# Batch norm on one core: a second DMA ring for the stores, parameters fetched as rows, and a last tile in two halves

## The chip, the cores and the metric

The kernel runs on one core of one Trainium2 chip. The metric is the device time of one execution in microseconds (us). The figure for the kernel before is the median of ten executions. The profile and the trace come from one of them, which has a time of its own.

## What is computed

The reference is batch normalisation with stored statistics over an input of 32 x 256 x 128 x 128 in float32:

```python
mean = running_mean.reshape(1, -1, 1, 1)
var = running_var.reshape(1, -1, 1, 1)
return gamma * (x - mean) / np.sqrt(var + eps) + beta
```

Each of 256 channels has one scale, gamma / sqrt(var + eps), and one shift, beta - mean * scale. The output is x * scale + shift, element by element. `x` is 537 MB and the output is as large, so 1074 MB pass through the core.

## The kernel before

The 256 channels are cut into two blocks of 128, one channel to a partition. With 32 images this makes 64 tiles of 128 x 16384 float32, 8.39 MB each, 64 KB in a partition. `xr[i]` and `outr[i]` are tile i in the input and in the output; tile i uses column i % 2 of the scales and shifts.

Three buffers of that size (`NBUF`, a pool of the tile framework, tag `t`) hold tiles. A tile is loaded into one, `compute` rewrites it in place on VectorE with one `tensor_scalar` (times scale, plus shift), and `store` writes it out from there. The framework places the semaphores: a load into a used buffer waits for the store that empties it, a `compute` for its load, a store for its `compute`.

Loads (line 48) and stores (line 97) are all issued by SyncE (SP), so they share one queue of the DMA hardware, in the order in which the program issues them. First come loads 0, 1 and 2. Then a loop goes over pairs of tiles (K = NBUF - 1 = 2):

```python
for i in idxs:
    compute(i)
for i in idxs:
    store(i)
for i in idxs:
    issue_load(i + NBUF)
```

SP's order is therefore L0 L1 L2, S0 S1, L3 L4, S2 S3, L5 L6 and so on (L a load, S a store), ending with L63, S62, S63.

The four parameter vectors of 256 values are fetched by four DMAs issued by GpSimd (POOL, line 56), each rearranged so that a partition gets its two channels' values: elements of 4 bytes. ScalarE takes the square root (line 71, with a table load ahead of it), VectorE the reciprocal, two products and a difference (lines 78 to 81). These give `scale_t` and `shift_t`, which tile 0 waits for.

Of the kernel before, what the change touches and what calls it, by code (L numbers as in the profile page):

```python
# [1 line left out]

# [4 lines left out]


SINGLE_QUEUE = True  # L10
NBUF = 3


@with_exitstack
def kernel(
    ctx: ExitStack,
    tc: tile.TileContext,
    x: bass.AP,
    gamma: bass.AP,
    beta: bass.AP,  # L20
    running_mean: bass.AP,
    running_var: bass.AP,
    out: bass.AP,
):
    nc = tc.nc
    eps = 1e-5

    N, C, H, W = x.shape
    P = nc.NUM_PARTITIONS
    assert C % P == 0  # L30
    NCB = C // P
    HW = H * W
    NT = N * NCB

    params = ctx.enter_context(tc.tile_pool(name="params", bufs=1))
    data = ctx.enter_context(tc.tile_pool(name="data", bufs=NBUF))

    xr = x.rearrange("n (cb p) h w -> (n cb) p (h w)", p=P)
    outr = out.rearrange("n (cb p) h w -> (n cb) p (h w)", p=P)

    tiles = {}
    loads = {}

    def issue_load(i):
        if i >= NT:
            return
        t = data.tile([P, HW], mybir.dt.float32, tag="t")
        loads[i] = nc.sync.dma_start(out=t[:], in_=xr[i])  # L48
        tiles[i] = t

    for i in range(NBUF):
        issue_load(i)

    def load_param(ap_1d):
        t = params.tile([P, NCB], mybir.dt.float32, tag=ap_1d.tensor.name)
        nc.gpsimd.dma_start(out=t, in_=ap_1d.rearrange("(j p) -> p j", p=P))  # L56
        return t

    var_t = load_param(running_var)
    gamma_t = load_param(gamma)  # L60
    beta_t = load_param(beta)
    mean_t = load_param(running_mean)

    eps_t = params.tile([P, 1], mybir.dt.float32, tag="eps")
    nc.vector.memset(eps_t, eps)  # L65

    scale_t = params.tile([P, NCB], mybir.dt.float32, tag="scale")
    shift_t = params.tile([P, NCB], mybir.dt.float32, tag="shift")
    tmp_t = params.tile([P, NCB], mybir.dt.float32, tag="tmp")

    nc.scalar.activation(  # L71
        out=tmp_t[:],
        in_=var_t[:],
        func=mybir.ActivationFunctionType.Sqrt,
        bias=eps_t[:],
        scale=1.0,
    )
    nc.vector.reciprocal(out=tmp_t[:], in_=tmp_t[:])  # L78
    nc.vector.tensor_mul(out=scale_t[:], in0=gamma_t[:], in1=tmp_t[:])  # L79
    nc.vector.tensor_mul(out=tmp_t[:], in0=mean_t[:], in1=scale_t[:])  # L80
    nc.vector.tensor_sub(out=shift_t[:], in0=beta_t[:], in1=tmp_t[:])  # L81

    def compute(i):
        t = tiles[i]
        cb = i % NCB
        nc.vector.tensor_scalar(  # L86
            out=t[:],
            in0=t[:],
            scalar1=scale_t[:, cb : cb + 1],
            scalar2=shift_t[:, cb : cb + 1],  # L90
            op0=mybir.AluOpType.mult,
            op1=mybir.AluOpType.add,
        )

    def store(i):
        t = tiles.pop(i)
        (nc.sync if SINGLE_QUEUE else nc.scalar).dma_start(out=outr[i], in_=t[:])  # L97

    K = NBUF - 1
    for b in range((NT + K - 1) // K):  # L100
        idxs = [i for i in range(K * b, K * b + K) if i < NT]
        for i in idxs:
            compute(i)
        for i in idxs:
            store(i)
        for i in idxs:
            issue_load(i + NBUF)


# [1 line left out]
_INS = ['x', 'gamma', 'beta', 'running_mean', 'running_var']  # L111
_OUTS = [((32, 256, 128, 128), 'float32')]


# [23 lines left out]
```

## Time and profile before

| | |
|---|---|
| median of ten executions | 2487.51 us (2486.53 to 2491.59) |
| the profiled execution's own time | 2486.91 us |
| its span in the profile | 2484.9 us |
| moved by DMA in the span | 1073.77 MB, 432 GB/s on average |
| `tensor_scalar` on VectorE, 128 x 16384 | 64 times, 8812 ns each |
| a load, from issue to landing (median) | 38.6 us |
| a store, from issue to landing (median) | 49.8 us |
| the four parameter fetches, from issue to landing | 10.9, 15.4, 19.7 and 21.7 us |

The span runs from the first to the last instruction that the profile counts; the execution's own time is 2.0 us longer, and the median of the ten is 0.6 us above that execution. The time from issue to landing contains the time in which a transfer stands in the queue behind others, so it is longer than the transfer itself. The page's row "GB/s" has one number for each fortieth of the span (62.1 us). In the chain of waits, a piece is named for the work whose end released the next step.

### The profile page before, as it was taken

Reading aid. Unit: us, or ns where it says so; the run is one execution under the profiler, and the core shown is the slowest. Engines: PE = TensorE matmul, PEld = TensorE weight load, DVE = VectorE, ACT = ScalarE, POOL = GpSimd, SP = SyncE. Lnnn points to the kernel's source line nnn. Section 1 sums busy time; section 2 is a strip of 40 time slices with the busy share of each in tenths; the row PEclk is TensorE's granted clock in tenths of the full one; section 3 lists DMA queues with packets and bytes.
Section 4 is the critical chain, followed back from the end, with each engine's and each line's share of the span. In section 5 each row is a group of like instructions: output and inputs, shape, how many; then the busy total and the mean of one; then the engine's idle time right before and its main releaser. Section 6 shows DMA issues by size and latency. Waiting matters only on the chain.

```text
span 2484.9 us, 378 instructions
## 1 busy us (share of the span) xinstructions
DVE 564.7 (23%) x69; ACT 1.6 (0%) x2; POOL 3.2 (0%) x8
## 2 busy tenths in 40 slices
DVE  2122211222112221122212222121221212222121
ACT  0000000000000000000000000000000000000000
POOL 0000000000000000000000000000000000000000
DMA  9999999999999999999999999999999999999999
GB/s 410 434 436 430 431 433 435 433 434 428 435 436 437 427 438 436 428 434 437 435 429 436 435 431 436 436 435 428 437 435 430 435 436 431 436 436 436 430 434 400
DMA packets 18562, 1073.77 MB, mean 432 GB/s; under 512 B 2176, under 2 KB 2176, under 8 KB 2176
## 3 DMA queue, kind: packets, MB, share of 16 engines
q1 hardware_dynamic: 18432, 1073.75, 99.9%
q0 software_dynamic: 128, 0.00, 0.0%
q14 instruction: 2, 0.02, 0.0%
HBM read 536.88 MB, written 536.87 MB: 432 GB/s over the span
## 4 chain that ended last, share of the span: by engine, by line
DMA 51%; another core or an unknown queue 36%; DVE 11%; SPq 0%; issue 0%; POOL 0%; DVEq 0%; POOLq 0%; PEldq 0%
DMA t<-in_x_dram 48%; DVE t L86 11%; DMA out_dram<-t 2%; DMA t<-in_running_mean_dram 1%; SPq L97 0%; POOL t L56 0%; DVEq L86 0%; POOLq L133 0%; SPq L48 0%; DVE shift_t L81 0%; DVE tmp_t L80 0%; DVEq L80 0%; PEldq L133 0%
## 5 line engine op out<-in xcount | busy, mean ns | idle before, releaser
L86 DVE TENSOR_SCALAR t<-t,scale_t,shift_t 128x16384 f32<-128x16384 f32 x64 | 564.0, 8812 | 1864.7 <-DMA t<-in_x_dram 1864.6
L78 DVE RECIPROCAL tmp_t<-tmp_t 128x2 f32<-128x2 f32 x1 | 0.2, 167 | 12.9 <-ACT tmp_t L71 12.9
L80 DVE TENSOR_TENSOR tmp_t<-t,scale_t 128x2 f32<-128x2 f32 x1 | 0.2, 161 | 7.5 <-DMA t<-in_running_mean_dram 7.5
L71 ACT ACT_TABLE_LOAD x1 | 1.3, 1283 | 12.2 <-DMA t<-in_running_var_dram 12.2
L79 DVE TENSOR_TENSOR scale_t<-t,tmp_t 128x2 f32<-128x2 f32 x1 | 0.2, 161 | 3.6 <-DMA t<-in_gamma_dram 3.6
L56 POOL DMA_DIRECT2D t<-in_running_var_dram x1 | 0.8, 837 | 0.8 <-PEq L133 0.8
L56 POOL DMA_DIRECT2D t<-in_gamma_dram x1 | 0.7, 722 | 0.0
L56 POOL DMA_DIRECT2D t<-in_beta_dram x1 | 0.7, 722 | 0.0
L56 POOL DMA_DIRECT2D t<-in_running_mean_dram x1 | 0.7, 722 | 0.0
L71 ACT ACTIVATE tmp_t<-t,eps_t 128x2 f32<-128x2 f32 x1 | 0.3, 297 | 0.0
L65 DVE MEMSET eps_t<- 128x1 f32 x1 | 0.1, 59 | 0.8 <-PEq L122 0.8
L81 DVE TENSOR_TENSOR shift_t<-t,tmp_t 128x2 f32<-128x2 f32 x1 | 0.2, 162 | 0.0
L122 POOL MEMSET const-bfloat16-1.0<- 128x1 bf16 x1 | 0.1, 96 | 0.0
L122 POOL MEMSET const-float32-0.0<- 128x1 f32 x1 | 0.1, 93 | 0.2 <-issue 0.2
L122 POOL MEMSET const-float32-1.0<- 128x1 f32 x1 | 0.1, 93 | 0.0
L122 POOL MEMSET const-uint8-127<- 128x1 uint8 x1 | 0.1, 93 | 0.0
## 6 DMA issues: line engine op xcount, KB each, us to landing
t<-in_x_dram SPq DMA_DIRECT2D x64, 38.6
out_dram<-t SPq DMA_DIRECT2D x64, 49.8
t<-in_running_var_dram POOLq DMA_DIRECT2D x1, 1.0 KB, 10.9
t<-in_gamma_dram POOLq DMA_DIRECT2D x1, 1.0 KB, 15.4
t<-in_beta_dram POOLq DMA_DIRECT2D x1, 1.0 KB, 19.7
t<-in_running_mean_dram POOLq DMA_DIRECT2D x1, 1.0 KB, 21.7
```

What stands on the lines that cost most here:

```text
L56: nc.gpsimd.dma_start(out=t, in_=ap_1d.rearrange("(j p) -> p j", p=P))
L65: nc.vector.memset(eps_t, eps)
L71: nc.scalar.activation(out=tmp_t[:], in_=var_t[:], func=mybir.ActivationFunctionType.Sqrt, bias=eps_t[:], scale=1.0,)
L78: nc.vector.reciprocal(out=tmp_t[:], in_=tmp_t[:])
L79: nc.vector.tensor_mul(out=scale_t[:], in0=gamma_t[:], in1=tmp_t[:])
L80: nc.vector.tensor_mul(out=tmp_t[:], in0=mean_t[:], in1=scale_t[:])
L81: nc.vector.tensor_sub(out=shift_t[:], in0=beta_t[:], in1=tmp_t[:])
L86: nc.vector.tensor_scalar(out=t[:], in0=t[:], scalar1=scale_t[:, cb : cb + 1], scalar2=shift_t[:, cb : cb + 1], op0=mybir.AluOpType.mult, ...
L122: nc = _bacc.Bacc("TRN2", target_bir_lowering=False, num_devices=1)
```

## The change

Loads stay on SP. Stores are issued by ScalarE (ACT), and so go into a second queue (ring) of the same DMA hardware. The whole body stands in one critical section (`tc.tile_critical`), inside which the program sets its own semaphores in place of the framework's: `loaded[s]` and `stored[s]` for each buffer s, and `done`, counted up by each `compute`. Load i waits until the store of tile i - 3 has landed, `compute` i for its load, store i for its `compute`. In the code there are no groups of loads and stores any more: each queue holds its own kind alone, in the order of the tiles.

The last tile, 63, is loaded, computed and stored in two halves of its rows (partitions 0 to 63, then 64 to 127), each half with a DMA, an instruction and a DMA of its own.

The parameters are fetched as four rows of 1 KB by ACT into a zeroed 32 x 256 tile `rows`, which VectorE transposes in 32 x 32 blocks (`turned`); four copies put the pieces into `par`, where partition p holds the four parameters of channels p and 128 + p. The arithmetic after that is the same, with an explicit wait between steps.

`fill` puts instructions that only count up an otherwise unused semaphore: 84 on SP between load 2 and load 3, 68 on ACT behind the four fetches, 52 on VectorE ahead of the transpose.

The core of the diff:

```diff
-SINGLE_QUEUE = True
 NBUF = 3
+FILL = {"sync": 84, "scalar": 68, "vector": 52}
...
-    for i in range(NBUF):
-        issue_load(i)
-    def load_param(ap_1d):
-        t = params.tile([P, NCB], mybir.dt.float32, tag=ap_1d.tensor.name)
-        nc.gpsimd.dma_start(out=t, in_=ap_1d.rearrange("(j p) -> p j", p=P))
-        return t
...
+    with tc.tile_critical():
+        def step(inst, sem=None, value=None):
+            if sem is not None:
+                inst._wait_ge(sem, value)
+            elif count[0]:
+                inst._wait_ge(vec, count[0])
+            inst.then_inc(vec, 1)
+            count[0] += 1
+            return count[0]
+        def fill(name):
+            for _ in range(FILL[name]):
+                getattr(nc, name).sem_inc(idle, 1)
+        last = NT - 1
+        half = [slice(0, P // 2), slice(P // 2, P)]
+        for i in range(NT):
+            s, turn = i % NBUF, i // NBUF
+            if i == NBUF:
+                fill("sync")
+            if i < last:
+                inst = nc.sync.dma_start(out=bufs[s][:], in_=xr[i]).then_inc(loaded[s], 16)
+                if turn:
+                    inst._wait_ge(stored[s], 16 * turn)
+            else:
+                for h in range(2):
+                    inst = nc.sync.dma_start(out=bufs[s][half[h]], in_=xr[i][half[h]]).then_inc(halves[h], 16)
+                    if h == 0:
+                        inst._wait_ge(stored[s], 16 * turn)
+        step(nc.vector.memset(eps_t[:], eps))
+        zeroed = step(nc.vector.memset(rows[:], 0.0))
+        for r, ap in enumerate((running_var, gamma, beta, running_mean)):
+            inst = nc.scalar.dma_start(out=rows[r : r + 1, :], in_=ap.rearrange("(o c) -> o c", o=1))
+            if r == 0:
+                inst._wait_ge(vec, zeroed)
+            inst.then_inc(fetched, 16)
+        fill("scalar")
+        fill("vector")
+        step(nc.vector.transpose(out=turned[:], in_=rows[:]), fetched, 64)
+        for q in range(NQ):
+            placed = step(nc.vector.tensor_copy(out=par[q * B : (q + 1) * B], in_=blocks[:, :, q, 0:4]))
...
     def store(i):
-        t = tiles.pop(i)
-        (nc.sync if SINGLE_QUEUE else nc.scalar).dma_start(out=outr[i], in_=t[:])
-    K = NBUF - 1
-    for b in range((NT + K - 1) // K):
...
+        def store(i, rows=slice(0, P)):
+            s = i % NBUF
+            return nc.scalar.dma_start(out=outr[i][rows], in_=bufs[s][rows]).then_inc(stored[s], 16)
+        for i in range(last):
+            compute(i)._wait_ge(loaded[i % NBUF], 16 * (i // NBUF + 1))
+            store(i)._wait_ge(done, i + 1)
+        for h in range(2):
+            compute(last, half[h])._wait_ge(halves[h], 16)
+            store(last, half[h])._wait_ge(done, last + h + 1)
+        for s in range(NBUF):
+            turns = (NT - s + NBUF - 1) // NBUF
+            nc.sync.wait_ge(stored[s], 16 * (turns + (1 if last % NBUF == s else 0)))
```

## The prediction, made before the result was known

> **What bounds the kernel now.** I read the busy rows and the DMA queues first, to see which unit is full, then the wait totals, to see who waits, then the chain of waits, to see how evenly the full unit runs. From the page:
>
> ```profile
> span 2484.9 us, 378 instructions
> DVE 564.7 (23%) x69; ACT 1.6 (0%) x2; POOL 3.2 (0%) x8
> ...
> DMA  9999999999999999999999999999999999999999
> GB/s 410 434 436 430 431 433 435 433 434 428 435 436 437 427 438 436 428 434 437 435 429 436 435 431 436 436 435 428 437 435 430 435 436 431 436 436 436 430 434 400
> ...
> q1 hardware_dynamic: 18432, 1073.75, 99.9%
> ...
> q14 instruction: 2, 0.02, 0.0%
> ```
>
> VectorE works 23% of the span; the 16 DMA engines are full in every slice and one queue holds them for 99.9%. Its 18432 packets are 144 for each of 128 transfers, so each engine gets nine: eight rows of 64 KB and one short packet. The wait totals say the same from the other side:
>
> ```profile
> DVE t L86 <- DMA t<-in_x_dram: 1864.6, 63, 49.6
> ...
> SPq L48 <- DMA out_dram<-t: 1480.9, 61, 30.1
> ```
>
> Neither wait is a loss in itself, since a transfer is always queued behind the one waited for. How evenly the queue runs is seen in the chain: a piece "DMA t<-in_x_dram" starts where a store has landed and frees a buffer, once per four transfers (two loads, two stores).
>
> ```profile
> 238.50 38.60 DMA t<-in_x_dram
> ...
> 316.38 38.54 DMA t<-in_x_dram
> ...
> 2020.22 38.51 DMA t<-in_x_dram
> ...
> 2097.45 38.58 DMA t<-in_x_dram
> ...
> 2406.79 38.58 DMA t<-in_x_dram
> ```
>
> The period is 316.38-238.50 = 77.88 us early and 2097.45-2020.22 = **77.23 us** late: 19.31 us a transfer. Over the 30 periods from 83.11 (also a piece of this chain) to 2406.79 it averages 77.456, so these hold 30 x 0.226 = 6.8 us over the best pace. Ahead of them, 83.11 us for four transfers is 5.9 over 77.23; about 3 of that is the issue at 0.74 us, the way to the first packet (at 1.75) and the landing (about 1.2, from the last packet's end at 2483.7 to the span's end), so some 3 us is slow running, while the parameters are fetched. The tail, 2484.9-2406.79 = 78.1, is four transfers and 0.9 us. **All that can be won is about 3+6.8+0.9 = 10.7 us, 0.4%.** The last store waits for nothing: load 63 lands at 2445.5, VectorE ends at 2454.3, and store 62 runs meanwhile.
>
> [...]
>
> **The change part by part**, summed against the profiled execution's 2484.9 us span. Its own time is 2486.91 (2.0 around the span); the median of the ten is 2487.51, 0.6 above.
>
> *Parameters.* Four issues leave POOL (0.84 + 3 x 0.72 us, ending 4.2 us) and four of about 0.34 us go onto ScalarE's queue, behind VectorE's memset. VectorE gains one memset, a 32x256 transpose and four copies; no row shows the transpose, the others resemble the 0.16 us rows, so the chain grows by 1 to 3 us. Behind it stand tile 0 and store 0. Cover: before, tile 0 starts at 25.68 and loads 1 and 2 keep the engines busy to 63.77, so some 29 us of lateness costs nothing; without it each us late is a us lost. Fewer tiny packets among the first loads give back part of the 3 slow us; bounds 0 to -2, I take -1.0.
>
> *Idle instructions.* 84 on SP, 68 on ScalarE, 52 on VectorE. The nearest row is SP's semaphore instruction at 17 ns: 1.4, 1.2 and 0.9 us. All stand ahead of a wait: SP's before load 3, which waits for store 0 (83 us before); the others before the parameters (11 to 22 us). Even at 100 ns each, 8.4 us, they stay covered: 0. They move two small instruction packets: 0.
>
> *Hand-placed semaphores.* A critical section adds barrier steps before load 0 and three waits at the end; bounds 0 to +1, I take +0.5. Load i+3 still waits for store i, and every later load stands behind that wait on SP; store i waits on ScalarE for tile i, with every later store behind it.
>
> *Two rings.* Stores leave SP, so a load no longer queues behind one; 64 stores at 0.34 us go to a queue that was idle. [...] a load and a store then share each engine row by row, and each takes twice 19.36 = 38.7 us. A buffer's round is 38.7+8.8+38.7 and some 5 for issues and landings, 91 us, against 3 x 38.7 = 116 for three tiles: 25 us of slack, neither ring runs dry, and the work remains 128 transfers. That is steady mixing, not phases of three and three. What a mixed row costs, the groups don't show. In the packet records the step from the last row of a load to the first of a store takes 2.506 us on average against 2.420 at the other joints between transfers, 0.086 more (2.6 us in 31 turns); the turns between 1764 and 2305 us, with the engines spread over 4.3 us, show none. Mixing makes 512 turns per engine. Bounds: -6.8 (best pace throughout) to 512 x 0.086 - 2.6 = +41. I take 0, since spread engines turned free.
>
> *Last tile in halves.* Two loads, two stores and two VectorE instructions instead of one each. The free size stays 16384, so VectorE takes 8.81 twice; the second half's compute is covered by stores 62 and the first half. Load 63 is released by store 60 and runs beside stores 61 and 62. The two half stores queue behind store 62 and have the engines alone. At full pace they take 2 x 9.66 = 19.3 us; at half pace [...] 2 x 19.3 = 38.6: **+19.3**. The half loads at half pace cost between 0 [...] and +19.3; I take +9.7. Sum of the item: 0 to +38.6, I take +29.0.
>
> Sum: 2484.9-1.0+0.5+0+29.0 = 2513.4 span; +2.0 = 2515.4; +0.6 = **2516 us**.
>
> **The rivals.** *A: [...]* (forecast), 2516, with 2506 to 2526 for the load term. For it: [...] nothing lies beside the last stores. Against it: no trace of this kernel shows it. Chance 0.42.
> *B: mixing costs.* With 0.086 us at each turn, +41 [...]: 2487.5+41-0.5 = 2528; with half that, 2507. For it: the slow turns up to 1700 us. Against it: the free ones after. Chance 0.30, of which 0.02 is too small to see.
> *C: faster.* The place is the turn from loads to stores. If both rings spread the engines so that no row waits, the 6.8 us go and the parameters give 1.0: 2487.5-6.8-1.0+0.5 = 2480; with half of the 6.8, 2483.6, no change. It decides only where the half rows cost under some 3 us. For it: 2020 to 2097 us already runs so. [...] Chance 0.28: 0.18 faster, 0.10 unchanged.
> *D: the second ring does nothing*, because the engines were full: inside C's unchanged part.
>
> **How the numbers follow.** 0.2%, 5 us, is about what a measurement of this kernel can tell from no change. Faster 0.18 (C). Same 0.10+0.02 = 0.12. Slower 0.42+0.28 = 0.70. The range runs from 2480 (C whole) to 2540 (A with half of B); A and B both in full, 2557, is left out, as is anything under C.
>
> **What would show it.** A: the GB/s row near 215 in the last 38 us, last half store landing 38 us after store 62. B: a lower GB/s row through all slices. C: 435 in all slices and a tail like before. Parameters right: tile 0 still starts by 26 us. Idle instructions right: no wait of load 3 or tile 0 ends on its own queue. The forecast is wrong if the last two half stores run at over 400 GB/s, or if the middle slices fall below 425.

## The result, and the profile after

The changed kernel takes **2531.13 us** (median of eight, 2528.67 to 2540.66) against 2488.51 us for the kernel before (median of 29 executions by then): ratio **1.0175, 95% interval 1.0166 to 1.0184**. Against the 2487.51 us that the forecast started from, it is 43.6 us slower; 28.5 were forecast. The executions of one two-ring kernel can lie over 20 us apart (2482 to 2506 us in one case below), so each profile below is read against its own execution. Ratios, here and below, are computed from all executions of both kernels, each version against the kernel before on the same chip, so they differ a little from the quotient of two medians.

The page of the changed kernel, the lines that answer to those shown of before:

```profile
span 2530.8 us, 470 instructions
DVE 574.9 (23%) x76; ACT 1.6 (0%) x2; POOL 0.2 (0%) x4
...
DMA  9999999999999999999999999999999999999996
GB/s 414 431 432 444 432 429 429 431 443 432 430 432 430 441 433 431 431 431 431 438 434 432 432 431 433 433 437 435 431 431 431 434 434 436 428 437 430 433 337 199
...
q1 hardware_dynamic: 9232, 536.88, 49.8%
q10 hardware_dynamic: 9240, 536.88, 49.5%
```

38 slices run at 428 to 444 GB/s (the first at 414), as before. The last two, 127 us, fall to 337 and 199, and in the one before last the DMA row still says 9: the engines are busy and move less. Two queues now share the time, 49.8% and 49.5%. The time went into the end.

The same in windows of 10 us (columns: window, its length, VectorE, ScalarE and POOL busy with the number of instructions, clock, busy share of the 16 DMA engines, GB/s; a packet counts in the window in which it starts, so a share can pass 1):

```profile
2000.00:2100.00 100.00, 26.44 (x3) 0.00 (x0) 0.00 (x0) 1.00 1.00 433
2400.00:2410.00 10.00, 0.00 (x0) 0.00 (x0) 0.00 (x0) 1.00 0.98 426
...
2430.00:2440.00 10.00, 6.28 (x1) 0.00 (x0) 0.00 (x0) 1.00 0.99 216
2440.00:2450.00 10.00, 0.00 (x0) 0.00 (x0) 0.00 (x0) 1.00 0.96 328
...
2490.00:2500.00 10.00, 0.13 (x1) 0.00 (x0) 0.00 (x0) 1.00 1.04 262
2500.00:2510.00 10.00, 0.00 (x0) 0.00 (x0) 0.00 (x0) 1.00 0.76 184
2510.00:2520.00 10.00, 0.00 (x0) 0.00 (x0) 0.00 (x0) 1.00 0.25 79
2520.00:2530.00 10.00, 0.00 (x0) 0.00 (x0) 0.00 (x0) 1.00 0.08 20
```

From 2430 to 2440 the engines are full (0.99) and move 216 GB/s in place of 433. After 2510 the rate falls because engines finish at different times: a share of 0.25 is four of 16 engines at work, 0.08 about one.

The timeline of that end (start, length, engine, line, operation; a row with x2 or x4 spans several instructions):

```profile
2396.84 93.80 ACTq L141 DMA_DIRECT2D out_dram<-t  x4
2416.95 1.54 SPq L95 DMA_DIRECT2D t<-in_x_dram  x2
2427.46 8.81 DVE L130 TENSOR_SCALAR t<-t,scale_t,shift_t 128x16384 f32<-128x16384 f32 x1 [30.66 <-DMA t<-in_x_dram]
2456.29 8.80 DVE L130 TENSOR_SCALAR t<-t,scale_t,shift_t 64x16384 f32<-64x16384 f32 x1 [20.02 <-DMA t<-in_x_dram]
2481.32 8.82 DVE L130 TENSOR_SCALAR t<-t,scale_t,shift_t 64x16384 f32<-64x16384 f32 x1 [16.22 <-DMA t<-in_x_dram]
```

The half loads are issued at 2416.95 and land at 2456.3 and 2481.3; the second half store follows at 2490.1 and ends at 2529. A half of the rows takes VectorE as long as a whole tile, 8.81 us.

The wait totals name the same releasers as before. One piece of the chain shows the pace with both rings at work: 2339.73 - 2300.92 = 38.81 us for a load and a store, 19.40 each.

```profile
2300.92 38.47 another core or an unknown queue
2339.73 38.54 another core or an unknown queue
```

The trace has a record of every packet with its start, length and size, though not with its engine. By these packet records, 123.67 transfers were done at 2400 us, against 123.79 in the kernel before: **2.3 us behind. The other 43 are lost after 2400.**

### The profile page after: what moved, and what is told of

Same layout as the page of the kernel before. It is cut to its first block, busy times and chain, and to the rows that moved or that the text cites. A ratio compares the mean times of both kernels' runs of the same rounds, so it can differ in the third digit from the quotient of the medians.

```text
span 2530.8 us, 470 instructions
## 1 busy us (share of the span) xinstructions
DVE 574.9 (23%) x76; ACT 1.6 (0%) x2; POOL 0.2 (0%) x4
## 3 DMA queue, kind: packets, MB, share of 16 engines
q1 hardware_dynamic: 9232, 536.88, 49.8%
q10 hardware_dynamic: 9240, 536.88, 49.5%
## 4 chain that ended last, share of the span: by engine, by line
another core or an unknown queue 92%; DMA 4%; DVE 1%; SPq 1%; issue 0%; ACTq 0%; ACT 0%; DVEq 0%
DMA out_dram<-t 2%; DMA t<-in_x_dram 2%; DVE t L130 1%; DMA rows<-in_running_mean_dram 1%; SPq L90 1%; ACTq L103 0%; DVE par L113 0%; DVE turned L109 0%; ACT std_t L115 0%; DVE rows L101 0%; DVE rstd_t L122 0%; DVE shift_t L125 0%; DVE ms_t L124 0%; DVE scale_t L123 0%
## 5 line engine op out<-in xcount | busy, mean ns | idle before, releaser
L130 DVE TENSOR_SCALAR t<-t,scale_t,shift_t 128x16384 f32<-128x16384 f32 (+1 forms) x65 | 572.8, 8813 | 1892.1 <-DMA t<-in_x_dram 1892.0
L115 ACT ACTIVATE std_t<-par,eps_t 128x2 f32<-128x2 f32 x1 | 0.3, 296 | 14.5 <-DVE par L113 14.5
```

What stands on the lines that cost most here:

```text
L115: nc.scalar.activation(out=std_t[:], in_=var_t, func=mybir.ActivationFunctionType.Sqrt, bias=eps_t[:], scale=1.0,)._wait_ge(vec, placed).t ...
L130: return nc.vector.tensor_scalar(out=bufs[s][rows], in0=bufs[s][rows], scalar1=scale_t[rows, cb : cb + 1], scalar2=shift_t[rows, cb : cb + 1],
```

## The experiments

Theories at the start: **half pace** (rows 0 to 63 or 64 to 127 alone move at half the pace of all 128, as the 216 GB/s of the window above would have it), against **drain** (two rings end on unevenly loaded engines however the last tile is cut). In the expectations of numbers 1 to 5 and 7, the case of half pace comes first.

**1. Tile 63 whole.** Loop and tail back to one load, one compute, one store; all else as changed.

```diff
-        for h in range(2):
-            compute(last, half[h])._wait_ge(halves[h], 16)
-            store(last, half[h])._wait_ge(done, last + h + 1)
+        compute(last)._wait_ge(loaded[last % NBUF], 16 * (last // NBUF + 1))
+        store(last)._wait_ge(done, last + 1)
```

> The changed kernel with tile 63 loaded, computed and stored whole; all else kept. [...] both terms of the tail go, and what remains is the two rings and the mixing, 2.3 us behind at 2400 us: about 2490 us, ratio 1.000 to 1.002. Drain (the two rings end on unevenly loaded engines however the last tile is cut): most of the 43 us stay, over 2515.

Measured: 2499.29 us, ratio 1.0049 (1.0036 to 1.0062). Three quarters of the loss go with the halves. But 11 us stay where I expected 2. The windows of this kernel:

```profile
2440.00:2450.00 10.00, 0.00 (x0) 0.00 (x0) 0.00 (x0) 1.00 1.00 433
2450.00:2460.00 10.00, 0.00 (x0) 0.00 (x0) 0.00 (x0) 1.00 0.82 354
2460.00:2470.00 10.00, 8.72 (x1) 0.00 (x0) 0.00 (x0) 1.00 0.06 26
2470.00:2480.00 10.00, 0.09 (x1) 0.00 (x0) 0.00 (x0) 1.00 0.97 419
```

While VectorE computes tile 63 (8.72 us), one engine of 16 works (0.06). Load 63 landed at 2461.3, and store 62 had ended on 15 engines by 2462. In the kernel before, store 62 stood behind load 63 in the one ring and covered that compute, from 2445.5 to 2454.3:

```profile
2446.00:2450.00 4.00, 4.00 (x1) 0.00 (x0) 0.00 (x0) 1.00 0.94 410
2450.00:2455.00 5.00, 4.31 (x1) 0.00 (x0) 0.00 (x0) 1.00 0.97 419
```

**2 and 3. Only the load, only the store in halves.** Number 2 keeps the two half loads, and VectorE waits for both and computes the tile whole; number 3 keeps the two half stores. (The remarks behind # tell the two edits apart.)

```diff
+        nc.vector.wait_ge(halves[0], 16)            # number 2
+        compute(last)._wait_ge(halves[1], 16)
+        store(last)._wait_ge(done, last + 1)
...
+        compute(last)._wait_ge(loaded[last % NBUF], 16 * (last // NBUF + 1))   # number 3
+        for h in range(2):
+            inst = store(last, half[h])
+            if h == 0:
+                inst._wait_ge(done, last + 1)
```

> The changed kernel with only the load of tile 63 in row halves; VectorE waits for both and computes the tile whole, the store is whole. [...] the packets of the half loads take 5.1 us in place of 2.4 when they meet, +15 us over the version with the tile whole, so about 2505. Drain: no more than 3 us over the version with the tile whole.

> The changed kernel with only the store of tile 63 in row halves (load and compute whole). [...] the two half stores have the engines alone and run at half pace, +20 to +30 us over the version with the tile whole, so 2510 to 2520. Drain: as the version with the tile whole, within 3 us.

Measured: 2514.07 us (1.0091, 1.0065 to 1.0117) and 2518.49 us (1.0109, 1.0090 to 1.0128). Over number 1, the half loads cost 14.8 us and the half stores 19.2 by the medians. These are good to some us only: each has four executions, with one low one (2499.44 and 2507.71), and the means give 10.4 and 15.1. In the packet records the median row of 64 KB takes 4.69 us in the half loads and 5.11 in the half stores, where 2.42 is usual. While the half stores of number 3 run alone, the engines are full and move half:

```profile
2490.00:2500.00 10.00, 0.00 (x0) 0.00 (x0) 0.00 (x0) 1.00 0.97 210
```

**4. Halves of columns.** `half` cuts 16384 columns into two; all 128 partitions stay in each.

```diff
-        half = [slice(0, P // 2), slice(P // 2, P)]
+        half = [slice(0, HW // 2), slice(HW // 2, HW)]
...
-                out=bufs[s][half[h]], in_=xr[i][half[h]]
+                out=bufs[s][:, half[h]], in_=xr[i][:, half[h]]
```

> The changed kernel with tile 63 in two halves of its columns instead of its rows: as many DMAs, bytes and waits, but all 128 partitions in each. [...] nothing is lost, about 2490, packets of 32 KB at 1.2 us. Drain or the number of transfers: about 2531, as in the changed kernel.

Measured: 2500.9 us (1.0046, 1.0032 to 1.0060): 30 us faster than row halves with as many DMAs. The packets of 32 KB take 1.21 us, full pace. It isn't at the 2490 expected and not faster than number 1, though compute and store of the last half are half as long. The second half lands at 2483.9 us, 65 us after the first was issued. Of its 16 shares, one for each engine, 14 had ended by 2456.9; the last two ended at 2483.5. From 2459 to 2477 these two start a load packet of 32 KB every 3.62 us, the time of one load packet (1.21) and one store packet of 64 KB (2.42): here the rings take turns packet by packet, which gives the smaller packets a third of the bytes.

**5. Row halves in one ring.** The kernel before, with tile 63 loaded and stored in row halves by SP.

```diff
-        loads[i] = nc.sync.dma_start(out=t[:], in_=xr[i])
+        parts = [slice(0, P // 2), slice(P // 2, P)] if i == NT - 1 else [slice(0, P)]
+        for r in parts:
+            loads[i] = nc.sync.dma_start(out=t[r], in_=xr[i][r])
...
```

> The kernel before (one ring) with the load and the store of tile 63 in row halves, computed whole. [...] half loads and half stores each have the engines alone in turn, packets of 5.1 us, +19.3 us for the load and +19.3 for the store: about 2526. If halves cost only where two rings interleave: within 5 us of the kernel before.

Measured: 2525.27 us (1.0156, 1.0143 to 1.0169), +37.9 against 38.6 expected. In one ring nothing mixes, and the pace is plain:

```profile
2400.00:2420.00 20.00, 0.00 (x0) 0.00 (x0) 0.00 (x0) 1.00 0.98 423
...
2430.00:2440.00 10.00, 0.00 (x0) 0.00 (x0) 0.00 (x0) 1.00 0.95 197
2440.00:2450.00 10.00, 0.00 (x0) 0.00 (x0) 0.00 (x0) 1.00 1.01 210
2450.00:2460.00 10.00, 0.00 (x0) 0.00 (x0) 0.00 (x0) 1.00 1.00 210
2460.00:2480.00 20.00, 8.81 (x1) 0.00 (x0) 0.00 (x0) 1.00 1.03 406
```

The half loads (2430 to 2460) move 197 to 210 GB/s on full engines; store 62, with 128 rows, follows at 406 in its window.

**6. Two rings alone.** The kernel before with `SINGLE_QUEUE = False`.

> The kernel before with its stores issued by ScalarE and nothing else changed. Uncovered compute (with two rings store 62 has ended when load 63 lands, so nothing runs while tile 63 is computed): about 2498, with some 10 us of empty DMA engines before the last store, as in the changed kernel with the tile whole. If the 11 us there came from the critical section, parameters or idle instructions: about 2488.

Measured: 2500.63 us (1.0035, 1.0017 to 1.0054). The second ring alone gives number 1's loss.

**7. Alternate rows.** Number 3 with even and odd rows in place of lower and upper ones.

```diff
-        half = [slice(0, P // 2), slice(P // 2, P)]
+        half = [slice(0, P, 2), slice(1, P, 2)]
```

> The changed kernel with tile 63 loaded and computed whole and stored in two halves of 64 rows each, even rows and odd rows in place of lower and upper rows. [...] the store costs what a whole one does, about 2499. If it is the number of rows or of DMAs that costs: 2518, as with lower and upper rows.

Measured: 2500.51 us (1.0042, 1.0029 to 1.0055), as with the store whole. The rows of the half stores take 2.42 to 2.47 us. In a window in which they run alone, they move twice what those of number 3 do:

```profile
2480.00:2490.00 10.00, 0.00 (x0) 0.00 (x0) 0.00 (x0) 1.00 1.03 446
```

As many rows and DMAs, other partitions: **it is the choice of the rows that costs (5.11 us a row in number 3, 2.42 to 2.47 here), not their number**, and the drain theory falls for the halves. Why adjacent rows are slow was not shown. One rival stands: with the partitions, the rows' places in DRAM changed too (64 KB pieces from all of the tile in place of one run of 4 MB), and no run here moves the one without the other.

**8. Store 62 held.** Number 1, with store 62 waiting on ScalarE until load 63 has landed, to give the compute its cover back.

```diff
+            if i == last - 1:
+                nc.scalar.wait_ge(loaded[last % NBUF], 16 * (last // NBUF + 1))
             store(i)._wait_ge(done, i + 1)
```

> The changed kernel with tile 63 whole, and store 62 held on ScalarE until load 63 has landed. Uncovered compute: load 63 shares the engines with less and lands some 19 us earlier, store 62 then covers the compute of tile 63, the empty 10 us go: 2487 to 2491. If the 11 us lie elsewhere: 2499, or later by the wait that is added.

Measured: 2501.14 us (1.0047, 1.0033 to 1.0060). The forecast failed; the windows say why:

```profile
2430.00:2440.00 10.00, 7.24 (x1) 0.00 (x0) 0.00 (x0) 1.00 0.97 419
2440.00:2450.00 10.00, 0.00 (x0) 0.00 (x0) 0.00 (x0) 1.00 0.39 170
2450.00:2460.00 10.00, 0.00 (x0) 0.00 (x0) 0.00 (x0) 1.00 0.06 26
2460.00:2470.00 10.00, 7.79 (x1) 0.00 (x0) 0.00 (x0) 1.00 0.73 315
```

From 2450 to 2460 one engine works and 15 have nothing left. Each engine closes its share of a transfer with a short packet of 4 bytes, and these are in the packet records: for load 63, 15 of them at 2443.2 to 2446.8 us, the last at **2461.9**. The compute of tile 63 starts at 2462.2: the load has landed when the slowest engine is done. In the kernel before, the shares of load 63 end within 4.0 us, 2441.1 to 2445.0; in number 1, from 2442.8 to 2460.9. Theory from here: **late engine** (with two rings an engine can fall behind the others, and loads land with it).

**9. One ring again.** Number 1 with all DMAs on SP, in the order of the kernel before; parameters, semaphores and idle instructions as changed.

```diff
-            return nc.scalar.dma_start(out=outr[i][rows], in_=bufs[s][rows]).then_inc(stored[s], 16)
+            return nc.sync.dma_start(out=outr[i][rows], in_=bufs[s][rows]).then_inc(stored[s], 16)
...
+        for b in range((NT + K - 1) // K):
+            idxs = [i for i in range(K * b, K * b + K) if i < NT]
+            for i in idxs:
+                compute(i)._wait_ge(loaded[i % NBUF], 16 * (i // NBUF + 1))
+            for i in idxs:
+                store(i)._wait_ge(done, i + 1)
+            for i in idxs:
+                if i + NBUF < NT:
+                    load(i + NBUF)
```

> The changed kernel with tile 63 whole and all loads and stores on SP's one ring, in the order of the kernel before; critical section, parameters as rows and idle instructions stay. If the second ring costs the 11 us (one DMA engine falls behind and load 63 lands late): about 2488, between 2485 and 2490. If the critical section, the parameters or the idle instructions cost them: about 2499.

Measured: 2490.22 us, ratio 1.0004 (0.9996 to 1.0013), the same as before. The 11 us belong to the second ring; the rest of the change costs nothing that can be measured (3 us at most, by the interval).

But an engine falls behind with one ring too. This profile is of the slowest of the 13 executions (2492.84 us). In it the shares of load 63 end from 2438.8 to 2450.8, 12.0 us apart and not 4.0. Store 62 stands behind load 63 on each engine and ends from 2458.1 on, so the compute of tile 63 (2451.2 to 2460.0) is covered all but its last 2 us:

```profile
2450.00:2460.00 10.00, 8.81 (x1) 0.00 (x0) 0.00 (x0) 1.00 0.86 374
2460.00:2470.00 10.00, 0.00 (x0) 0.00 (x0) 0.00 (x0) 1.00 1.00 433
```

So a late engine alone does not set the two-ring kernels apart. In the profiles of numbers 1, 3, 6, 7 and 8 the shares of load 63 end further apart, 18.1 to 22.9 us, and nothing stands behind load 63 on the engines that are done with it.

**10. Store 62 on SP's ring, behind load 63.**

```diff
-            return nc.scalar.dma_start(out=outr[i][rows], in_=bufs[s][rows])
+            return (nc.sync if i == last - 1 else nc.scalar).dma_start(out=outr[i][rows], in_=bufs[s][rows])
```

> The changed kernel with tile 63 whole, and store 62 issued by SP right behind load 63, so that each engine takes it after its own share of that load, without a wait for the others. One engine behind the others: its own share still ends 4 to 15 us late, and the time stays over the kernel before, 2490 to 2500. The order of store 62 and load 63 alone: 2484 to 2488, as in an execution without a late engine.

Measured: 2501.36 us (1.0048, 1.0035 to 1.0060; single executions 2493.79 to 2502.97), just above the late-engine end and clear of the other. In its profile, of the fastest of the five executions, two engines are late, 2451.6 against 2437.9 to 2441.1 for the other 14. Those 14 end store 62 at 2457.2 to 2460.4, so the compute (2452.1 to 2460.9) is nearly covered, and store 63 at 2481.3; the two late ones end it at 2490.3. What the other four executions lost, 2500.70 us and more, no profile shows.

**11. Tile 63 out in quarters of columns.** Loaded whole, then computed and stored in four pieces, to shorten the uncovered compute.

```diff
+        for h in range(4):
+            cols = slice(h * W4, (h + 1) * W4)
+            nc.vector.tensor_scalar(out=bufs[s][:, cols], in0=bufs[s][:, cols], ...).then_inc(done, 1)
+            nc.scalar.dma_start(out=outr[last][:, cols], in_=bufs[s][:, cols]).then_inc(stored[s], 16)._wait_ge(done, last + h + 1)
```

> The changed kernel with tile 63 loaded whole, then computed and stored in four quarters of its columns, all 128 partitions in each. Uncovered compute of tile 63: the first quarter's store starts 6.6 us sooner (three quarters of 8.81), so 6.6 us under the version with the tile whole, about 2493. If the compute is covered: no change, about 2499.

Measured: 2499.68 us (1.0032, 1.0016 to 1.0048), a miss for 2493 and no evidence for 6.6 us. Its single executions run from 2482.28 to 2506.32, and the profiled one took 2482.64 us. That gives the counterpart, an execution without a late engine:

```profile
2445.68 9.38 DVE L145 TENSOR_SCALAR t<-t,scale_t,shift_t 128x4096 f32<-128x4096 f32 x4 [29.70 <-DMA t<-in_x_dram]
2448.12 7.31 ACTq L153 DMA_DIRECT2D out_dram<-t  x4
```

Load 63 lands at 2445.7, not at 2461. All 16 shares end between 2442.6 and 2445.3, store 62 runs until 2459.8, and the compute is covered. At 2400 us 124.00 transfers were done, 4 us ahead of the kernel before. Between 100 and 2400 us, 14 load rows of 64 KB took over 2.48 us; in the profile of the changed kernel 379 did, and 7 store rows.

Such executions are not single ones: in numbers 6, 7, 8 and 11 together, 14 of 72 took 2482 to 2485 us, less than any execution of the kernel before beside them (2485.36 and up), and most of the others 2497 to 2507. Only this one of the 14 has a profile, so that they all lack a late engine is likely and not shown.

No version beat the kernel before in its median.

## Why the prediction was right in direction and short in size

- **Last tile in halves, +29.0: right in sum.** In the packet records after 2400 us, the rows of the changed kernel take 28.5 us for each engine more than they would at the usual 2.42 us a row: 14.3 in the half loads (9.7 forecast, within 0 to 19.3), the rest in the stores (19.3 forecast). That the two errors cancel is luck. That half rows run at half pace (rival A) was the author's assumption, which no trace of the kernel before shows; number 5 does, at 197 to 210 GB/s for 423. The half stores didn't have the engines alone: the first was free to go at 2465.1, when VectorE had done the first half, and the second half load landed at 2481.3. By the same reckoning it is 20.6 us in number 3 for the half stores alone, 19.3 in number 2 for the half loads (with the stores beside them), not 9.7, and 36.6 in number 5 for both in one ring.
- **Two rings, 0: the step that failed.** "Neither ring runs dry, and the work remains 128 transfers" holds for the sum over the engines: 2.3 us behind at 2400. The 38.7 us for a load beside a store, an estimate, came as 38.81. The step took the 16 engines as one. A load lands with its slowest engine (last share at 2461.9, compute at 2462.2, number 8), and in every profile with two rings and a whole last load, but number 11's, one to three engines ended their share of load 63 some 8 to 18 us after the rest. Load 63 then lands about when store 62 ends (where store 62 was not moved or held), nothing covers the compute of tile 63, and the late engine ends its stores late too. Measured: 11.4 us in number 1 (2499.29 less the 2487.92 beside it), 13.2 in number 6.
- In the changed kernel's own records this shows as idle time: between 2400 us and the last packet's end (2529.1) an engine is idle for 16.7 us on average, and 2.2 in the kernel before, whose last packet ends at 2483.7. The idle time, 14.5 us more, with 28.5 for the slow rows and the 2.3 before, makes 45.3 of the 45.4 us between the two ends. Number 1, without halves, has 15.5 us idle and 0.1 for slow rows. Some of the idle time can belong to the halves: number 5, with them in one ring, has 7.4.
- **Parameters, semaphores, idle instructions, -0.5 together: right within what can be told**, by number 9. The timeline has the terms:

```profile
0.95 116.95 SPq L90 DMA_DIRECT2D t<-in_x_dram  x5
2.73 0.32 ACTq L103 DMA_DIRECT2D rows<-in_running_mean_dram  x1
8.33 1.28 ACT L115 ACT_TABLE_LOAD   x1 [8.33 <-issue]
22.85 0.43 DVE L109 STREAM_TRANSPOSE turned<-rows 32x256 f32<-32x256 f32 x1 [21.40 <-DMA rows<-in_running_mean_dram]
25.30 8.81 DVE L130 TENSOR_SCALAR t<-t,scale_t,shift_t 128x16384 f32<-128x16384 f32 x1
```

  The first load starts 0.2 us later than before (0.95 for 0.74), tile 0 at 25.30 for 25.68. From the end of the fetches' issue (3.05) to the table load are 5.3 us for 68 idle instructions, 78 ns each; the wait for the parameters covers them, as forecast. By the packet records 4.95 transfers were done at 100 us, 4.94 before: that is 0.2 us gained, not 1.0.
- **Rival B, mixing at +41: wrong.** 2.3 us behind at 2400 us, after some 7600 load rows between store rows. **Rival C, 2480: not for the change as it is** (2528.67 us at the least). Without half rows by lower and upper partitions, two rings come near it, at 2482 to 2485, in about one execution of five (numbers 6, 7, 8 and 11), and number 11's profile shows one, without a late engine. The forecast reached 2540 by adding half of B to A; what came on top of A was no mixing but the idle end, which no rival named.
- The signs named: 215 GB/s in the last 38 us came as 242, 262, 184, 79 and 20, as the engines end apart; middle slices stayed over 425, as the forecast wanted.

What stays open is why an engine falls behind. The slow rows are nearly all loads, there are few of them in the execution without a late engine, and the packet records don't name the engine. Their number alone doesn't tell: the kernel before has 213, nearly all the last row of a load ahead of a store, and a spread of 4.0 us; number 1 has 97 and a spread of 18.1. In the one with store 62 held, the last shares of loads ended 3.5 us after the first at 200 us and 17.5 at 1517 us, in number 9 1.8 and 9.3, so the delay builds up on the way. Nothing was tried that would prevent it.

## What to carry to other kernels

A full DMA row with a low GB/s row (0.99 and 216 GB/s) meant a bad shape of transfer here: cut a tile along its columns (1.21 us for a packet of 32 KB, number 4), or into alternate rows (2.42 to 2.47 us for 64 KB, tried for stores, number 7), not into its lower and upper partitions (5.1 us, number 5). A load landed with its slowest engine (2461.9 us, the other 15 by 2446.8, number 8), so ask what covers the last compute if one engine is a packet or six late. The one ring, whose order puts a ready store behind the last load, gave that cover for nothing, even with engines 12 us apart (number 9, 2490.22 us); the same order of these two in SP's ring, with the other stores in a second one, did not bring the time back (number 10, 2501.36 us). And when a sum over engines shows no loss, look at the spread between them before costing a tail at zero.

## What the runs showed of the hardware that was not expected

- Stores of 64 alternate partitions moved at full pace (2.42 to 2.47 us a row of 64 KB, number 7), transfers of 64 adjacent ones at half, loads and stores alike (5.1 us, number 5). The half loads of 4 MB moved 197 to 210 GB/s there.
- Two rings shared an engine packet by packet, not byte by byte: loads of 32 KB (1.21 us) beside stores of 64 KB (2.42 us) started every 3.62 us (number 4). A row was a packet: q1 of the changed kernel, with 65 loads, has 9232, which is 8192 rows and 65 x 16 short ones.
- Engines drifted apart while all were busy (share 1.00 or 1.01 in each 100 us from 100 to 2400 in the kernel before). From the first to the last share of load 63 it is 4.0 us in the kernel before and 12.0 in number 9, both with one ring, and with two 2.7 (number 11) to 22.9 (number 3).
